# Layer 1's attention: one product of the ends of blocks 0 and 3 on GpSimd, and the gate multiplied last

## The chip, the core and the metric

The kernel runs on one core of a Trainium2 chip. A core has five engines that run side by side, each in its own order: TensorE (PE in the profile; PEld is its weight load), VectorE (DVE), ScalarE (ACT), GpSimd (POOL) and SyncE (SP). TensorE writes to PSUM, an accumulator memory in banks of 128 partitions x 512 fp32; all else is kept in SBUF. The metric is the device time of one execution in microseconds (us); the kernel before has a median of 3536.51 us over 3 runs (3531.72 to 3536.86).

## The reference, cut to what matters

Two layers over 2048 latent tokens on a 32 x 64 grid with 256 context tokens, model width 1024. The change lies in the second layer (layer 1): neighbourhood attention with 16 heads of 64, in which each query sees a window of 8 rows x 16 columns of the grid and all context tokens, then a gate.

```python
s_lat = einsum('bqhd,brkhd->bhqrk', qr, kb) * scale + bias        # window, with a table of biases
s_ctx = einsum('bqhd,bchd->bhqc', qr, k_ctx) * scale
p = softmax(concatenate([s_lat, s_ctx], -1))
o = einsum('bhqk,bkhd->bqhd', p_lat, vb) + einsum('bhqc,bchd->bqhd', p_ctx, v_ctx)
y = dot(o.reshape(..., 1024) * silu(z_x), w_out)
```

All is fp32. The projections and scores are computed with operands split into a high and a low part (names with h and l).

## The kernel before

Layer 1's attention (function odd_attention) works on one pair of the 16 heads at a time: eight turns j = 0 to 7, which this text calls heads 0 to 7. Queries are 4 blocks of 512 tokens (8 rows of the grid). In a head, 24 units follow each other: 8 for the context tokens (two per block) and 16 key tiles of 128 latent tokens (n = 0 to 15). A unit is

- eight score matmuls of TensorE (L1785) into a PSUM tile "st" of two banks; there are 2 such tiles, so that the scores of the next unit but one can only start when these have been read,
- for a key tile, additions of the bias table on VectorE (L1963), one to six of them for parts of the tile, from PSUM into an SBUF tile "opt" (11 of these),
- the exponential on ScalarE (L108, a helper through which all of ScalarE's work goes),
- some units later, the matmuls with the values into the output banks "o" (L1797 for context, L1815 for key tiles; 4 banks, one per block), and the sums of the exponentials "oacc" over key tiles, which GpSimd adds up (L1821; L1806 for the context, on VectorE for blocks 0 and 2, on GpSimd for 1 and 3).

When the last key tile of a block has been added, finish_blocks ends the block: TensorE sums oacc over the partitions (L1838, into an "st" tile), and ScalarE copies the result to an SBUF tile dc. From dc, which is minus twice the denominator, ScalarE makes rc, an approximate reciprocal by logarithm and exponential (tiles rl and opt). VectorE then takes four steps of 128 x 512:

- L1848: ln = dc x rc, both operands in SBUF,
- L1850: rc = rc x Z, both in SBUF, where Z is the gate (tiles os4 and ogate),
- L1854: o = (ln + 2) x o, in the output bank in PSUM; the factor ln + 2 corrects the reciprocal by one Newton step,
- L1855: rc = o x rc, from PSUM into SBUF.

A DMA issued by GpSimd (L1856) writes rc to HBM (RT1); the output projection after head 7 reads it.

finish_blocks is a generator: the attention loop takes one step of it per unit, so that its steps stand between those of the units. A scheduler then orders the instructions of each engine. Block 3 of a head is ended in the middle of the next head, and block 0 some 8 us later in its own head, so both ends stand close together. Block 2 of the head before is ended some 9 us ahead of its block 3, and block 1 of the head some 18 us behind its block 0. In head 7, blocks 2 and 3 are ended together, and VectorE and ScalarE also split the weights of the output projection.

Of the kernel before, what the change touches and what calls it, by code (L numbers as in the profile page):

```python
# [13 lines left out]
ALU = mybir.AluOpType  # L14
# [74 lines left out]
class Kern:  # L89
# [1630 lines left out]
    def odd_attention(self, out, pools, left, wout):  # L1720

        nc = self.nc
        self.RT1 = self.scr("RT1", (KD, P, SEQ), F32)
        NR, NC = (len(b) for b in BLOCKS["k"])
        with ExitStack() as es:
# [62 lines left out]
            def sums(acc, bb, n=1):  # L1788

                return [acc[bb // 2][:, i].rearrange("p r c -> p (r c)")[:, (bb % 2) * 512 : (bb % 2) * 512 + n * 512] for i in range(2)]  # L1790
# [41 lines left out]
            def finish_blocks(bbs, j, O, acc):  # L1832

                n, hf, o0 = len(bbs), bbs[0] // 2, bbs[0] % 2 * 512
                den = both()
                for b, bb in enumerate(bbs):
                    for i, a in enumerate(sums(acc, bb)):
                        mm = nc.tensor.matmul(den[i * 64 : i * 64 + 64, b, :], self.mtwos[:], a, start=True, stop=True)  # L1838
                dc = exps()
                self.act(dc[:, :n], den[:, :n])  # L1840
                yield mm
                ln = self.tl(lp, [P, 2, 512], "rl", bufs=1)
                self.act(ln[:, :n], dc[:, :n], AF.Ln, scale=-1.0)
                yield
                rc = exps()
                self.act(rc[:, :n], ln[:, :n], AF.Exp, scale=-1.0)
                yield
                nc.vector.tensor_tensor(out=ln[:, :n], in0=dc[:, :n], in1=rc[:, :n], op=ALU.mult)  # L1848
                flat = rc[:, :n].rearrange("p b c -> p (b c)")
                nc.vector.tensor_tensor(out=flat, in0=flat, in1=Z[j, hf][:, o0 : o0 + n * 512], op=ALU.mult)  # L1850
                yield
                for b, bb in enumerate(bbs):
                    o = O.pop(bb)[:].rearrange("p r c -> p (r c)")
                    nc.vector.scalar_tensor_tensor(out=o, in0=ln[:, b], scalar=2.0, in1=o, op0=ALU.add, op1=ALU.mult)  # L1854
                    nc.vector.tensor_tensor(out=rc[:, b], in0=o, in1=rc[:, b], op=ALU.mult)  # L1855
                (nc.sync if (j, bbs) == (7, [0]) else nc.gpsimd).dma_start(self.RT1[j, :, bbs[0] * 512 : (bbs[0] + n) * 512], flat)  # L1856

            def weights():

# [27 lines left out]
            Q, K, V, Z, tabs, raw = {}, {}, {}, {}, {}, {}  # L1887
# [15 lines left out]
            def flush(n):  # L1903

                mm = None
                for f, *a in pend[:n]:
                    mm = f(*a)
                del pend[:n]
                for x in late:
                    x[0] -= 1  # L1910
                for x in [x for x in late if x[0] <= 0]:
                    late.remove(x)
                    ends.append(finish_blocks(*x[1:]))
                    mm = next(ends[-1])
                    if x[1] == [0]:
                        for _ in ends.pop():
                            pass
                return mm
# [9 lines left out]
            for j in range(8):  # L1928
                OA[j] = {}, {}
                for s, (kind, n, u) in enumerate(units):  # L1930
                    g, c = divmod(n, 4)
# [21 lines left out]
                    else:  # L1953
# [7 lines left out]
                        for ro, ri, rn in pieces("k", 0, g, r0_, nr):  # L1961
                            for co, ci, cn in pieces("k", 1, c, c0, w):
                                bias = nc.vector.tensor_tensor(out=pt[:, :, ro : ro + rn, co : co + cn],  # L1963
                                                               in0=ps[:, :, ro : ro + rn, d + co : d + co + cn],
                                                               in1=tabs[j][:, :, ri : ri + rn, ci : ci + cn], op=ALU.add)
# [260 lines left out]
```

## Time and profile before

| | us |
|---|---|
| median of 3 runs (lowest, highest) | 3536.51 (3531.72, 3536.86) |
| the profiled execution's own time | 3539.31 |
| its span, first to last instruction | 3537.5 |
| layer 1's attention in it | about 2967 to 3364 |
| the output projection behind it | to the end |

The profile is of one execution. A row of a group shows line, engine, operation, output<-inputs by the program's names, shapes and count, then the total busy time in us and the mean of one in ns, then the idle time of the engine just ahead of these instructions and what ended it. A row of the order of time begins with start and length in us; in brackets stand the idle time ahead of it and its releaser, and x16 counts equal instructions in a row. In a row of a stretch of time, the busy time of each engine is followed by its count of instructions, and then come the clock granted to TensorE (1.00 is full speed), the busy share of the DMA engines and GB/s. Names of tiles stand without their buffer numbers.

### The profile page before, as it was taken

The numbers are of one execution on the slowest core, as the hardware profiler recorded it, in microseconds if no ns is written. First come the engines' busy times: TensorE is split into PE (matmuls) and PEld (weight loads), VectorE is DVE, ScalarE is ACT, GpSimd is POOL, SyncE is SP. The second block draws the span as 40 slices with busy tenths as digits, with TensorE's granted clock in tenths as the row PEclk, the third lists the DMA queues.
The fourth block names the chain that finished last, engine by engine and source line by source line (L and its number), as shares of the span: only waits on it lengthen the run. The fifth ranks groups of instructions, "written<-read, shape, count | busy, mean of one in ns | idle before, by whom it ended". The sixth has DMA issues, their size and how long they took to land. (4 is left out here: it accounts for less than half of the span.)

```text
span 3537.5 us, 54848 instructions
## 1 busy us (share of the span) xinstructions
PE 3442.3 (97%) x20228; PEld 2663.8 (75%) x20228; DVE 2438.7 (69%) x4522; ACT 1465.6 (41%) x2612; POOL 1052.0 (30%) x1295
## 2 busy tenths in 40 slices
PE   7999999999999999999999999999999999999899
PEld 6888987888896666665557878888788887555577
DVE  4677755888886777768876655455577884666865
ACT  4545552111113554546664344445422223555532
POOL 1343331111111333422211133333111114767611
PEclk9999999999999999999999999999999999999999
DMA  7555555233325242334525674445754546555374
GB/s 252 142 163 160 149 142 152 96 108 94 89 79 168 62 134 80 104 112 134 177 84 140 133 202 154 130 143 164 251 161 141 163 142 213 198 192 198 99 182 63
DMA packets 350111, 508.40 MB, mean 144 GB/s; under 512 B 32666, under 2 KB 233066, under 8 KB 342884
## 3 DMA queue, kind: packets, MB, share of 16 engines
q1 hardware_dynamic: 297364, 386.91, 35.9%
q0 software_dynamic: 29456, 82.14, 8.8%
q10 hardware_dynamic: 23024, 35.85, 3.0%
q8 instruction: 160, 2.62, 0.3%
q14 instruction: 107, 0.88, 0.1%
HBM read 325.99 MB, written 196.60 MB: 148 GB/s over the span
## 5 line engine op out<-in xcount | busy, mean ns | idle before, releaser
L706 DVE TENSOR_REDUCE mm<-mx 128x1 f32<-128x512 f32 (+1 forms) x656 | 389.3, 628 | 85.2 <-PE mx L705 78.2
L108 ACT ACTIVATE apt<-st 128x1024 f32<-128x1024 f32 (+1 forms) x296 | 300.2, 1015 | 303.2 <-PE st L1175 283.4
L1182 DVE TENSOR_TENSOR acc<-acc,apt 128x1024 f32<-128x1024 f32 x256 | 341.0, 1332 | 82.5 <-ACT apt L108 63.8
L1175 PE MATMUL st<-aq,akh 64*128 64x512 f32 x1728 | 312.0, 408 | 1.2 <-ACT apt L108 0.9
L1085 PE MATMUL av<-apt,av 128*64 128x512 f32 x1152 | 265.8, 598 | 0.0
L1821 POOL TENSOR_TENSOR oacc<-oacc,opt 128x528 f32<-128x528 f32 (+4 forms) x192 | 230.3, 1217 | 71.0 <-ACT opt L108 65.1
L705 PE MATMUL mx<-mk,mq 96*128 96x512 f32 (+1 forms) x656 | 236.0, 373 | 4.8 <-DMA mq<-QC 4.6
L1175 PE MATMUL st<-aq,akl 64*128 64x512 f32 (+1 forms) x1152 | 230.6, 390 | 0.0
L108 ACT ACTIVATE u<-gm 128x352 f32<-128x352 f32 (+1 forms) x140 | 68.6, 497 | 375.0 <-PE gm L133 207.1
L1703 DVE CUSTOM_DVE_ANT_1 mx<-mx,mtab 128x105 f32<-128x105 f32 (+14 forms) x576 | 183.1, 340 | 48.5 <-PE mx L1697 35.8
L1175 PEld LDWEIGHTS st<-aq,akh 64*128 64x128 f32 x1728 | 152.7, 185 | 82.7 <-ACT apt L108 28.8
L1963 DVE TENSOR_TENSOR opt<-st,tab 128x496 f32<-128x496 f32 (+16 forms) x288 | 124.5, 484 | 107.8 <-PE st L1785 106.1
L1085 PEld LDWEIGHTS av<-apt,av 128*64 128x64 f32 x1152 | 76.3, 136 | 135.3 <-issue 133.6
L108 ACT ACTIVATE opt<-opt 128x930 f32<-128x930 f32 (+9 forms) x130 | 104.5, 806 | 161.2 <-DVE opt L1963 155.1
L705 PEld LDWEIGHTS mx<-mk,mq 96*128 96x128 f32 x656 | 121.6, 189 | 17.0 <-issue 5.1
L1175 PEld LDWEIGHTS st<-aq,akl 64*128 64x128 f32 (+1 forms) x1152 | 112.1, 184 | 22.9
L1785 PE MATMUL st<-qh,kh 64*128 64x512 f32 (+6 forms) x384 | 85.1, 438 | 32.1 <-DVE opt L1963 25.8
L1785 PEld LDWEIGHTS st<-qh,kh 64*128 64x128 f32 x384 | 37.7, 190 | 102.4 <-issue 48.6
L220 POOL TENSOR_TENSOR oss<-oss,mhalf 128x8 f32<-128x8 f32 x68 | 112.6, 1656 | 5.4
L1552 DVE TENSOR_TENSOR onat<-gm,oss 128x512 f32<-128x512 f32 x68 | 46.9, 690 | 95.8 <-POOL oss L220 95.8
L131 PE MATMUL gm<-w1h,hhi 128*128 128x512 f32 x280 | 112.0, 400 | 0.2 <-ACT ovz L108 0.2
L133 PE MATMUL gm<-w1h,hlo 128*128 128x512 f32 x280 | 110.0, 393 | 0.0
(778 smaller groups left out, 9724.6 us busy)
## 6 DMA issues: line engine op xcount, KB each, us to landing
H<-x ACTq DMA_DIRECT2D x32, 512.0 KB
adaw<-ada_w SPq DMA_DIRECT2D x64, 256.0 KB
wraw<-w_od SPq DMA_DIRECT2D x64, 256.0 KB
K1t<-okt POOLq DMA_DIRECT2D x16, 1024.0 KB, 6.6
x<-H SPq DMA_DIRECT2D x31, 512.0 KB
mtab<-rpb_q SPq DMA_DIRECT2D x16, 899.0 KB
x<-xin SPq DMA_DIRECT2D x18, 512.0 KB
x<-xin POOLq DMA_DIRECT2D x18, 512.0 KB, 5.3
```

The lines of the kernel that those rows point to most:

```text
L108: return self.nc.scalar.activation(out, in_, func, **kw)
L131: self.nc.tensor.matmul(out, lh(k), rh(k), start=start and j == 0, stop=False)
L220: return g.tensor_tensor(out=out, in0=out, in1=self.mhalf[:, : shp[1]], op=ALU.pow)
L705: mm = nc.tensor.matmul(ps[:, :w], q[:A_QK, (t % 6) * P : (t % 6) * P + P], k[:A_QK, k0 : k0 + w], start=True, stop=True)
L706: nc.vector.tensor_reduce(out=m[:, t, n : n + 1], in_=ps[:, :w], axis=AX.X, op=ALU.max)
L1085: mm = nc.tensor.matmul(O[j, nb][i * 64 : i * 64 + 64, :w], V[j, kt // TT][:, kt % TT, i * 64 : i * 64 + 64], pts[:, i, :w], start=n == 0, ...
L1175: mm = nc.tensor.matmul(ps[:, o // 64, :w], k[o : o + r, kb, kq], Q[o : o + r, qb, :w], start=m == 0, stop=m == 4)
L1182: added = nc.vector.tensor_tensor(out=acc[:, :, :w], in0=a[:, :, :w], in1=pts[:, :, :w], op=ALU.add)
L1703: nc.vector.tensor_tensor_reduce(out=s, in0=s, in1=tb[:, ri : ri + rn, ci : ci + cn], scale=1.0, scalar=-3e38, op0=ALU.add, op1=ALU.max, a ...
L1785: mm = nc.tensor.matmul(ps(i), ones[s] if k is None else k[s, ks], qs(q[s]), start=n == 0, stop=n == 3)
L1821: nc.gpsimd.tensor_tensor(out=a, in0=a, in1=pts[:, :, a0 - r0 : a1 - r0, :], op=ALU.add)
L1963: bias = nc.vector.tensor_tensor(out=pt[:, :, ro : ro + rn, co : co + cn], in0=ps[:, :, ro : ro + rn, d + co : d + co + cn], in1=tabs[j][: ...
```

## The change

For blocks 0 and 3 of heads 0 to 6, which are 14 of the 31 block ends, the product ln = dc x rc is issued on GpSimd instead of VectorE. In all block ends the gate's product is taken out of its place ahead of the two steps on the output bank. Instead the bank is first multiplied by rc in place, and the gate is multiplied last, out of the bank into rc.

```diff
-                nc.vector.tensor_tensor(out=ln[:, :n], in0=dc[:, :n], in1=rc[:, :n], op=ALU.mult)
-                flat = rc[:, :n].rearrange("p b c -> p (b c)")
-                nc.vector.tensor_tensor(out=flat, in0=flat, in1=Z[j, hf][:, o0 : o0 + n * 512], op=ALU.mult)
+                near = nc.gpsimd if bbs in ([0], [3]) and j < 7 else nc.vector
+                near.tensor_tensor(out=ln[:, :n], in0=dc[:, :n], in1=rc[:, :n], op=ALU.mult)
                 yield
                 for b, bb in enumerate(bbs):
                     o = O.pop(bb)[:].rearrange("p r c -> p (r c)")
                     nc.vector.scalar_tensor_tensor(out=o, in0=ln[:, b], scalar=2.0, in1=o, op0=ALU.add, op1=ALU.mult)
-                    nc.vector.tensor_tensor(out=rc[:, b], in0=o, in1=rc[:, b], op=ALU.mult)
-                (nc.sync if (j, bbs) == (7, [0]) else nc.gpsimd).dma_start(self.RT1[j, :, bbs[0] * 512 : (bbs[0] + n) * 512], flat)
+                    nc.vector.tensor_tensor(out=o, in0=o, in1=rc[:, b], op=ALU.mult)
+                    nc.vector.tensor_tensor(out=rc[:, b], in0=o, in1=Z[j, hf][:, o0 + b * 512 : o0 + b * 512 + 512], op=ALU.mult)
+                (nc.sync if (j, bbs) == (7, [0]) else nc.gpsimd).dma_start(self.RT1[j, :, bbs[0] * 512 : (bbs[0] + n) * 512], rc[:, :n].rearrange("p b c -> p (b c)"))
```

In the changed kernel the first product is line L1849, the three steps on the bank are L1853, L1854 and L1855, and the DMA stays L1856. The order of TensorE's and ScalarE's instructions stays as it was. On VectorE, where block 3 of head 1 is ended in the middle of head 2 (rl_29205 is ln, opt_29189 dc, opt_29219 rc, ogate the gate, o_28845 the bank; the first L1963 rows are the bias of the key tile ahead, opt_29283 that of the next):

```order
 L1963 TENSOR_TENSOR opt_29227<-st_29226,tab_28558 128x2x15x16
 L1963 TENSOR_TENSOR opt_29227<-st_29226,tab_28558 128x2x15x7
-L1848 TENSOR_TENSOR rl_29205<-opt_29189,opt_29219 128x512
-L1850 TENSOR_TENSOR opt_29219<-opt_29219,ogate_29024 128x512
-L1854 SCALAR_TENSOR_TENSOR o_28845<-rl_29205,o_28845 128x512
-L1855 TENSOR_TENSOR opt_29219<-o_28845,opt_29219 128x512
+L1853 SCALAR_TENSOR_TENSOR o_28845<-rl_29205,o_28845 128x512
+L1854 TENSOR_TENSOR o_28845<-o_28845,opt_29219 128x512
+L1855 TENSOR_TENSOR opt_29219<-o_28845,ogate_29024 128x512
 L1963 TENSOR_TENSOR opt_29283<-st_29282,tab_28558 128x2x15x8
 L1963 TENSOR_TENSOR opt_29283<-st_29282,tab_28558 128x2x15x16
```

VectorE goes straight from the bias to L1853, which needs GpSimd's ln, and the next bias stands behind the three steps. A little later on VectorE, at the end of block 0 of head 2 (rl_29317 is ln, os4 the gate, o_29058 the bank):

```order
 L1963 TENSOR_TENSOR opt_29327<-st_29326,tab_28558 128x2x465
-L1848 TENSOR_TENSOR rl_29317<-opt_29315,opt_29319 128x512
 L1963 TENSOR_TENSOR opt_29339<-st_29338,tab_28558 128x2x465
-L1850 TENSOR_TENSOR opt_29319<-opt_29319,os_5038_29158 128x512
-L1854 SCALAR_TENSOR_TENSOR o_29058<-rl_29317,o_29058 128x512
-L1855 TENSOR_TENSOR opt_29319<-o_29058,opt_29319 128x512
+L1853 SCALAR_TENSOR_TENSOR o_29058<-rl_29317,o_29058 128x512
+L1854 TENSOR_TENSOR o_29058<-o_29058,opt_29319 128x512
+L1855 TENSOR_TENSOR opt_29319<-o_29058,os_5038_29157 128x512
 L1963 TENSOR_TENSOR opt_29356<-st_29355,tab_28558 128x2x15x16
```

The second 2 x 465 bias now follows the first one directly, ahead of everything that needs ln. On GpSimd, the changed kernel's order from the end of block 3 of head 1 to the end of block 0 of head 2 (oacc_5010 and oacc_5045 are the sums of blocks 0, 1 and of blocks 2, 3 of head 2):

```order
L1821 TENSOR_TENSOR oacc_5010_29008<-oacc_5010_29008,opt_29208 128x2x11x31
L1821 TENSOR_TENSOR oacc_5045_29203<-oacc_5045_29203,opt_29192 128x2x4x31
L1849 TENSOR_TENSOR rl_29205<-opt_29189,opt_29219 128x512
L1821 TENSOR_TENSOR oacc_5010_29008<-oacc_5010_29008,opt_29227 128x2x11x23
L1821 TENSOR_TENSOR oacc_5045_29203<-oacc_5045_29203,opt_29208 128x2x4x31
L1821 TENSOR_TENSOR oacc_5045_29203<-oacc_5045_29203,opt_29227 128x2x4x23
L1856 DMA RT<-opt_29219 128x512
L1806 TENSOR_TENSOR oacc_5045_29203<-opt_29241,opt_29272 128x2x512
L1821 TENSOR_TENSOR oacc_5010_29008<-oacc_5010_29008,opt_29283 128x2x3x24
L1821 TENSOR_TENSOR oacc_5045_29203<-oacc_5045_29203,opt_29283 128x2x12x24
L1849 TENSOR_TENSOR rl_29317<-opt_29315,opt_29319 128x512
L1821 TENSOR_TENSOR oacc_5010_29008<-oacc_5010_29008,opt_29327 128x2x3x31
```

The two L1849 rows are new; the DMA L1856 stood ahead of the 2 x 4 x 23 addition before, and all other rows keep their order.

## The prediction

> **What bounds the kernel now.** I read the busy time of the stage that the change touches first, then its groups by shape, and last its order of time around the places where TensorE stands still. In layer 1's attention TensorE is busy for 364.56 of 397 us (the first number after the comma; VectorE's is the third, GpSimd's the fifth, the granted clock 0.96):
>
> ```profile
> 2967.00:3364.00 397.00, 364.56 (x3161) 224.22 (x3161) 268.59 (x433) 220.05 (x298) 282.43 (x237) 0.96 0.51 182
> ```
>
> So a microsecond saved on VectorE or GpSimd counts only where TensorE waits for it. Groups by shape (count, busy time, mean ns, idle time of the engine ahead and who ended it) show one such place:
>
> ```profile
> L1785 PE MATMUL st<-qh,kh 64*128 64x264 f32 x32 | 6.7, 416 | 14.9 <-DVE opt L1963 14.9
> L1848 DVE TENSOR_TENSOR rl<-opt,opt 128x512 f32<-128x512 f32 x30 | 48.1, 1604 | 37.6 <-ACT opt L108 37.6
> L1855 DVE TENSOR_TENSOR opt<-o,opt 128x512 f32<-128x512 f32 x32 | 22.0, 690 | 0.9
> ```
>
> The score matmuls of one key tile waited 14.9 us for VectorE's bias addition L1963. And L1848, the product that the change moves, takes 1604 ns on average, while L1855, as large but with one operand in PSUM, takes 690. The order of time in the middle of head 2, where block 3 of head 1 and then block 0 of head 2 are finished (start, length):
>
> ```profile
> 3083.97 1.50 POOL L1821 TENSOR_TENSOR oacc<-oacc,opt 128x682 f32<-128x682 f32 x1
> 3084.38 1.64 DVE L1848 TENSOR_TENSOR rl<-opt,opt 128x512 f32<-128x512 f32 x1
> 3085.43 1.13 POOL L1821 TENSOR_TENSOR oacc<-oacc,opt 128x248 f32<-128x248 f32 x1
> 3086.51 1.63 POOL L1821 TENSOR_TENSOR oacc<-oacc,opt 128x506 f32<-128x506 f32 x1
> 3087.03 0.68 DVE L1854 SCALAR_TENSOR_TENSOR o<-rl,o 128x512 f32<-128x512 f32 x1
> 3087.74 0.69 DVE L1855 TENSOR_TENSOR opt<-o,opt 128x512 f32<-128x512 f32 x1
> 3088.09 0.66 POOL L1821 TENSOR_TENSOR oacc<-oacc,opt 128x248 f32<-128x248 f32 x1
> 3088.35 0.96 DVE L1963 TENSOR_TENSOR opt<-st,tab 128x240 f32<-128x240 f32 x2
> 3088.73 0.55 POOL L1856 DMA_DIRECT2D RT<-opt  x1
> 3089.30 0.56 POOL L1821 TENSOR_TENSOR oacc<-oacc,opt 128x184 f32<-128x184 f32 x1
> 3089.34 0.81 ACT L108 ACTIVATE opt<-opt 128x720 f32<-128x720 f32 x1 [1.19 <-DVE opt L1963]
> 3089.80 2.39 POOL L1806 TENSOR_TENSOR oacc<-opt,opt 128x1024 f32<-128x1024 f32 x1
> 3090.00 0.49 PE L1785 MATMUL st<-qh,kh 64*128 64x480 f32 x2
> 3090.12 0.60 ACT L108 ACTIVATE opt<-st 128x512 f32<-128x512 f32 x1
> 3092.15 3.95 POOL L1821 TENSOR_TENSOR oacc<-oacc,opt 128x144 f32<-128x144 f32 x4
> 3092.25 4.40 DVE L1848 TENSOR_TENSOR rl<-opt,opt 128x512 f32<-128x512 f32 x1
> 3092.61 1.41 POOL L1821 TENSOR_TENSOR oacc<-oacc,opt 128x576 f32<-128x576 f32 x1
> 3096.57 1.11 DVE L1963 TENSOR_TENSOR opt<-st,tab 128x930 f32<-128x930 f32 x1
> 3097.74 0.39 PE L1785 MATMUL st<-qh,kh 64*128 64x264 f32 x2 [2.98 <-DVE opt L1963]
> 3098.44 3.02 PE L1815 MATMUL o<-opt,ov 128*64 128x72 f32 x24
> ```
>
> At 3092.25 L1848 stands still for 4.40 us: GpSimd's four additions end at 3096.10 (3092.15 + 3.95) and only then does it run its usual 0.6. The bias addition behind it comes at 3096.57, and TensorE sits idle for 2.98 us until its score bank is read. L1854 and L1855, with one operand in PSUM, take 0.68 and 0.69 beside a running GpSimd. Five heads have this gap (5 x 2.98 = 14.9); heads 0 and 5 have smaller ones there:
>
> ```profile
> 3003.80 0.43 PE L1785 MATMUL st<-qh,kh 64*128 64x352 f32 x2 [1.57 <-DVE opt L1963]
> 3244.47 0.43 PE L1785 MATMUL st<-qh,kh 64*128 64x352 f32 x2 [0.78 <-DVE opt L1963]
> 3256.58 0.50 PE L1785 MATMUL st<-qh,kh 64*128 64x512 f32 x2 [0.93 <-DVE opt L1963]
> ```
>
> There is a second price. Right behind each of the five gaps the granted clock (third number from the end) is 0.50 (the first and fourth of five stretches, and their sum):
>
> ```profile
> 3050.56:3053.97 3.41, 3.41 (x28) 2.74 (x24) 2.30 (x8) 1.40 (x2) 3.39 (x5) 0.50 0.17 65
> ...
> 3193.92:3200.74 6.82, 5.83 (x44) 4.76 (x46) 4.54 (x11) 2.38 (x3) 4.69 (x6) 0.50 0.10 38
> ...
> sum 23.89, PE 21.56 PEld 17.23 DVE 17.69 ACT 9.03 POOL 17.66; mean PE 4.31 PEld 3.45 DVE 3.54 ACT 1.81 POOL 3.53
> ```
>
> **The change, part by part.**
>
> 1. Block 0's L1848 leaves VectorE (heads 0 to 6). The 4.40 us go, and the second 930-wide L1963 now stands ahead of the wait. Gain on TensorE: the five gaps, 14.9 us.
>
> 2. With them goes the halved clock. TensorE was busy for 21.56 us at half speed; at full speed that is 10.8. Gain 10.8; 0 if another idle stretch halves the clock there again.
>
> 3. What takes their place: VectorE is in order, and L1853 now waits for the GpSimd product L1849, with the next bias additions queued behind it. L1849's length is not in this trace. The nearest rows are GpSimd's products of the same shape in layer 0:
>
> ```profile
> L1010 POOL TENSOR_TENSOR rc<-rc,azt 128x512 f32<-128x512 f32 x16 | 20.7, 1292 | 129.2 <-DVE rc L1008 129.2
> L850 POOL TENSOR_TENSOR gat<-gat,ge 128x512 f32<-128x512 f32 x18 | 36.6, 2032 | 112.7 <-DVE gat L848 112.7
> 2991.67 1.16 POOL L1821 TENSOR_TENSOR oacc<-oacc,opt 128x506 f32<-128x506 f32 x1
> ```
>
> I take 1.29 (the lower bound is 1.16, a slightly narrower addition); 2.03 is the upper end, from a line that runs beside VectorE products, while here VectorE will be waiting. The Trainium skill says, in "GPSIMD Engine Reference", section 3.1, that an fp32 tensor-tensor takes GpSimd about twice VectorE's time (1.96x); 1292 against 690 here is 1.87x, and 1.96 x 690 would make it 1.35 and the sum below 0.8 us worse.
>
> Block 3, in head 2's times. GpSimd's 682 ends at 3085.47. Its 248 is no longer disturbed (0.66 instead of 1.13): 3086.14. L1849: 3087.46. Three VectorE steps (0.71, 0.71, 0.61 from start to start; the third multiplies the gate out of PSUM and is priced as L1855) end at 3089.55, where L1963 began at 3088.35 before: 1.2 later. It ends near 3090.55, TensorE wanted its bank at 3090.00 and waits 0.6. ScalarE's 0.81 and then 0.60 move to 3092.0, which holds the second score tile by another 0.4. GpSimd gets back 0.47 on the 248 and 0.47 on the 506 (1.16, not 1.63), which pays most of L1849.
>
> Block 0: GpSimd goes on from 3087.46 with 1.16, 0.66, 0.56, a DMA issue of 0.55, 2.39, then the 144 and 576 wide additions (0.46 to the 576's start, and 1.41), then L1849: 3096.1. Three steps end at 3098.2, the next L1963 pair at 3099.2. TensorE, 1.0 late, now at full clock, has run the 264-wide tile and its 24 matmuls (3.02 becomes 1.6) by 3098.1 and waits 1.1 to 1.2. Together 2.2 us a head, in six heads (1 to 6): 13.2 us lost. The bounds: none of it, if GpSimd runs ahead by that much; 13.2 + 14 x 0.74 = 23.6 with 2.03, since each of the 14 products (two in each of seven heads) moves a TensorE wait by its own length.
>
> 4. Head 0 has block 0 alone: 1.57 becomes some 0.5, a gain of 1.1. Head 5's 0.78 and 0.93 fall under point 3's waits: gain 1.7.
>
> 5. Head 7 ends block 3 of head 6. There a gap of 2.04 follows an L1848 among VectorE's weight work:
>
> ```profile
> 3341.68 0.49 PE L1785 MATMUL st<-qh,kh 64*128 64x480 f32 x2 [2.04 <-DVE opt L1963]
> ```
>
> Part of it goes; against it the output bank is held one step (0.69) longer for the gate. I take 0, with 2 us either way.
>
> 6. The gate product itself: one VectorE step out, one in, 0.69 each. In blocks 1 and 2 it moves behind the bias addition, hidden as before by TensorE. The DMA of L1856 moves behind one 0.56 addition on GpSimd; layer 1's outputs are read only at the end: 0.
>
> Sum: -14.9 - 10.8 + 13.2 - 1.1 - 1.7 + 0 = -15.3 us. Against the profiled execution's 3539.31 that is 3524.0; the median of the runs is 2.8 lower, so 3521.2.
>
> **A rule weighed.** In the trace 1.59 us of idle TensorE in a 3.42 us stretch (1.83 busy) left the clock at 1.00 and 1.64 (1.77 busy) was followed by 0.50:
>
> ```profile
> 3313.38:3316.80 3.42, 1.83 (x14) 0.81 (x14) 2.85 (x5) 3.06 (x5) 2.65 (x3) 1.00 0.35 129
> 3340.69:3344.10 3.41, 1.77 (x14) 1.32 (x16) 3.41 (x4) 2.44 (x4) 3.39 (x3) 1.00 0.20 77
> 3344.10:3347.52 3.42, 3.42 (x13) 0.98 (x10) 3.42 (x3) 0.90 (x2) 1.52 (x2) 0.50 0.70 219
> ```
>
> The new waits are 0.6 + 0.4 together and 1.2 alone, under that. The Trainium skill ("TensorE: Matmul & The Clock Gate", section "Why this matters for your kernels") asks only for no idle gaps over about 3 us; by that the 2.98 us gaps would cost no clock, which is rival E's sum, within 0.2%. The trace disagrees with it: all five gaps of 2.98 are followed by 0.50.
>
> **Rivals.** 0.2%, or 7 us, is about what a measurement of this kernel tells from no change.
> - A, no change. L1849 takes 2.03, as in L850's row: 14 x 0.74 = 10.4 us more, -4.9: 3531.6. For it: such a row exists. Against: 1292 in sixteen products of the same form.
> - B, slower: the new waits halve the clock. It decides once block 3's waits pass 1.6 us in one stretch of 3.4: with 2.03 they are 1.7. Then each of six heads loses half of 3.4 to 6.8 us, 1.7 to 3.4, on top of A: +5 to +15, 3542 to 3552.
> - C, better: GpSimd's queue has slack that I don't see and the new waits vanish: -28.5, 3508.
> - D, the change does not do what it says: the 4.40 are not GpSimd's doing, and block 0's steps in PSUM stall as long: -1, 3535. Against it stand L1855's mean of 690 above and L1854 (minimum, median, maximum in ns):
>
> ```profile
> L1854 DVE SCALAR_TENSOR_TENSOR o<-rl,o x32: 681/683/691, 3001.4 to 3386.5; 128x512 f32<-128x512 f32 x32
> ```
>
> - E, the halved clock has another cause than the gaps and stays: point 2 is 0, -15.3 + 10.8 = -4.5, 3532. Against it: the clock rows just above.
>
> **How the numbers follow.** Forecast (-22 to -8) 0.68, A 0.10, B 0.06, C 0.10, D 0.03, E 0.03. Faster: forecast, C and the near edge of A, 0.80; same 0.14; slower 0.06. The range reaches from near C to A's 3531.6: 3509 to 3532; the forecast's own is 3514.5 to 3528.5.
>
> **What would show it.** L1849 on GpSimd 14 times at 1.2 to 1.4 us; no 4.4 us on VectorE; the 14.9 of the 264-wide score tile gone, with waits of 0.4 to 1.2 for L1963 at the 480- and 352-wide tiles; clock 1.00 from 3045 to 3290; heads 3 us shorter. I am wrong if L1849 is over 1.7, or if clock 0.50 still follows the middle of a head.

## The result and the profile after

The changed kernel takes 3519.81 us in the median of 5 runs (3519.53 to 3523.02), the kernel before 3536.51 in 5 runs beside it (3531.72 to 3536.86). The ratio is 0.9959, with a 95% interval of 0.9944 to 0.9973: 16.7 us faster (14.5, at the middle of that ratio), and the prediction was 15.3 faster, 3521.2.

The profiled execution took 3519.81 with a span of 3518.0, which is 19.5 less than the span before. Not all of it lies where the change is. The groups of one line give the start of the first and of the last of the score matmuls L1785; before:

```profile
L1785 PE MATMUL st<-qh,kh x384: 281/443/660, 2967.2 to 3364.0; 64*128 64x512 f32 x64, 64*128 64x360 f32 x32, 64*128 64x480 f32 x32, 64*128 64x288 f32 x16
```

and after:

```profile
L1785 PE MATMUL st<-qh,kh x384: 278/432/766, 2961.5 to 3345.0; 64*128 64x512 f32 x64, 64*128 64x360 f32 x32, 64*128 64x480 f32 x32, 64*128 64x288 f32 x16
```

Layer 1's attention begins 5.7 us earlier, in code that the change doesn't touch; that part differs by some us from one execution to the next (2958.9 to 2967.5 in the eleven traces of this study). So all traces are compared below by **the stage**, from the first L1785 to the end of the span: 570.4 us before (3537.5 - 2967.2) and 556.6 after, 13.8 less, against the 15.3 of the prediction's sum. Up to the last score matmul of head 7 the two traces have TensorE's and ScalarE's instructions in the same order; behind it, in the output projection, some of them have changed places.

The busy times of the engines in the attention after (order of columns as in the prediction's first row: TensorE, its weight load, VectorE, ScalarE, GpSimd, then the granted clock):

```profile
2961.00:3345.50 384.50, 356.63 (x3169) 219.71 (x3169) 235.06 (x419) 220.45 (x298) 292.56 (x251) 0.98 0.54 188
```

VectorE is 33 us less busy (268.59 before), GpSimd 10 us more, and TensorE's clock is 0.98 instead of 0.96. Two groups of score matmuls by shape before (busy, mean ns, then the idle time ahead and who ended it):

```profile
L1785 PE MATMUL st<-qh,kh 64*128 64x480 f32 x64 | 14.9, 459 | 4.7 <-DVE opt L1963 2.6 <-ACT opt L108 1.3
L1785 PE MATMUL st<-qh,kh 64*128 64x352 f32 x32 | 8.0, 491 | 6.2 <-DVE opt L1963 6.2
```

and the groups after:

```profile
L1849 POOL TENSOR_TENSOR rl<-opt,opt 128x512 f32<-128x512 f32 x14 | 18.5, 1319 | 0.0
L1849 DVE TENSOR_TENSOR rl<-opt,opt 128x512 f32<-128x512 f32 x16 | 15.4, 963 | 36.8 <-ACT opt L108 36.8
L1853 DVE SCALAR_TENSOR_TENSOR o<-rl,o 128x512 f32<-128x512 f32 x32 | 22.0, 689 | 33.9 <-POOL rl L1849 33.9
L1785 PE MATMUL st<-qh,kh 64*128 64x480 f32 x64 | 15.4, 474 | 7.8 <-DVE opt L1963 6.8 <-ACT opt L108 0.5
L1785 PE MATMUL st<-qh,kh 64*128 64x352 f32 x32 | 7.2, 432 | 13.5 <-DVE opt L1963 13.5
L1785 PE MATMUL st<-qh,kh 64*128 64x264 f32 x32 | 5.5, 338 | 0.7 <-DVE opt L1963 0.7
```

The 14.9 us at the 264-wide score tile are 0.7. In their place TensorE waits longer at the 352-wide tile (13.5 for 6.2) and the 480-wide one (7.8 for 4.7); heads 1 to 6 have 8.6 and 5.5 of these waits, and had 0.8 at each before. Ahead of them VectorE's L1853 waits for GpSimd's product (33.9). Rows from the order of time in the middle of head 2, the same place as in the prediction:

```profile
3076.96 1.29 POOL L1849 TENSOR_TENSOR rl<-opt,opt 128x512 f32<-128x512 f32 x1
3078.28 0.70 DVE L1853 SCALAR_TENSOR_TENSOR o<-rl,o 128x512 f32<-128x512 f32 x1 [3.55 <-POOL rl L1849]
3079.82 0.69 DVE L1855 TENSOR_TENSOR opt<-o,ogate 128x512 f32<-128x512 f32 x1
3080.42 0.96 DVE L1963 TENSOR_TENSOR opt<-st,tab 128x240 f32<-128x240 f32 x2
3081.53 0.49 PE L1785 MATMUL st<-qh,kh 64*128 64x480 f32 x2 [0.85 <-DVE opt L1963]
...
3082.73 2.37 DVE L1963 TENSOR_TENSOR opt<-st,tab 128x930 f32<-128x930 f32 x2 [1.34 <-PE st L1785]
3083.75 1.87 POOL L1821 TENSOR_TENSOR oacc<-oacc,opt 128x144 f32<-128x144 f32 x2
3085.56 1.29 POOL L1849 TENSOR_TENSOR rl<-opt,opt 128x512 f32<-128x512 f32 x1
3086.89 0.69 DVE L1853 SCALAR_TENSOR_TENSOR o<-rl,o 128x512 f32<-128x512 f32 x1 [1.79 <-POOL rl L1849]
3089.03 1.74 DVE L1963 TENSOR_TENSOR opt<-st,tab 128x480 f32<-128x480 f32 x6
3090.11 0.43 PE L1785 MATMUL st<-qh,kh 64*128 64x352 f32 x2 [1.42 <-DVE opt L1963]
```

The 4.40 us are gone, and each product on GpSimd is followed, some 2 us later, by a TensorE wait: 0.85 behind block 3, 1.42 behind block 0.

### The profile page after: what moved, and what is told of

Its sections match the earlier page's. It is cut to its first block, busy times and chain, and to the rows that moved or that the text cites. A ratio compares the mean times of both kernels' runs of the same rounds, so it can differ in the third digit from the quotient of the medians.

```text
span 3518.0 us, 54816 instructions
## 1 busy us (share of the span) xinstructions
PE 3431.9 (98%) x20228; PEld 2656.4 (76%) x20228; DVE 2405.5 (68%) x4509; ACT 1466.8 (42%) x2612; POOL 1061.2 (30%) x1309
## 4 chain that ended last, share of the span: by engine, by line
PE 78%; DVE 6%; POOL 5%; DMA 5%; ACT 3%; issue 2%; SPq 1%; DVEq 0%; ACTq 0%; POOLq 0%
PE gm L133 10%; PE gm L131 10%; PE gm L132 10%; PE st L1175 10%; PE av L1085 7%; PE mx L705 4%; PE st L1785 2%; PE pu L1364 2%; PE o L1364 2%; POOL oacc L1821 2%; PE st L1364 1%; PE pj L1364 1%; PE mx L1697 1%; PE o L1815 1%; DMA adaw<-ada_w 1%
## 5 line engine op out<-in xcount | busy, mean ns | idle before, releaser
L1821 POOL TENSOR_TENSOR oacc<-oacc,opt 128x528 f32<-128x528 f32 (+4 forms) x192 | 221.6, 1171 | 48.1 <-ACT opt L108 42.7
L1963 DVE TENSOR_TENSOR opt<-st,tab 128x496 f32<-128x496 f32 (+16 forms) x288 | 124.3, 485 | 94.6 <-PE st L1785 93.6
L705 PEld LDWEIGHTS mx<-mk,mq 96*128 96x128 f32 x656 | 121.6, 189 | 17.5 <-issue 5.3
L1785 PE MATMUL st<-qh,kh 64*128 64x512 f32 (+6 forms) x384 | 83.4, 429 | 27.4 <-DVE opt L1963 22.7
L131 PE MATMUL gm<-w0h,hhi 128*128 128x512 f32 x272 | 109.6, 403 | 0.0
```

Source lines behind the costliest of these rows:

```text
L131: self.nc.tensor.matmul(out, lh(k), rh(k), start=start and j == 0, stop=False)
L705: mm = nc.tensor.matmul(ps[:, :w], q[:A_QK, (t % 6) * P : (t % 6) * P + P], k[:A_QK, k0 : k0 + w], start=True, stop=True)
L1821: nc.gpsimd.tensor_tensor(out=a, in0=a, in1=pts[:, :, a0 - r0 : a1 - r0, :], op=ALU.add)
```

## The experiments

All are edits of the changed kernel but one, which says so. The table takes the stage apart, from the trace of each: the length of head 0, of heads 1 to 6 and of head 7 (from the first L1785 of a head to that of the next, for head 7 to its last), and the remainder to the end. In heads 1 to 6, *idle* is the sum of TensorE's idle times over 0.05 us, *half* is half of its busy time in stretches with a granted clock of 0.50, and *rest* is what is left of the length.

| us | stage | head 0 | heads 1-6 | idle | half | rest | head 7 | to the end |
|---|---|---|---|---|---|---|---|---|
| before | 570.4 | 41.4 | 291.5 | 17.6 | 10.8 | 263.0 | 64.4 | 173.0 |
| changed | 556.6 | 40.6 | 280.6 | 14.8 | 1.7 | 264.1 | 62.9 | 172.5 |
| 1 gate last, no GpSimd | 563.7 | 40.7 | 290.0 | 17.5 | 11.4 | 261.0 | 60.5 | 172.4 |
| 2 gate first, GpSimd | 596.8 | 40.6 | 317.5 | 41.5 | 13.5 | 262.5 | 65.6 | 173.0 |
| 3 block 0 alone | 548.6 | 40.5 | 274.1 | 10.5 | 1.7 | 261.8 | 60.4 | 173.6 |
| 4 block 3 alone | 567.9 | 40.6 | 293.6 | 23.0 | 6.8 | 263.8 | 61.3 | 172.3 |
| 5 additions left out | 537.6 | 40.2 | 263.8 | 2.2 | 0.0 | 261.7 | 61.4 | 172.2 |
| 6 VectorE, in steps | 570.4 | 40.8 | 296.8 | 21.9 | 13.9 | 261.1 | 60.5 | 172.3 |
| 7 both, in steps | 553.2 | 40.9 | 278.3 | 12.9 | 0.0 | 265.4 | 61.5 | 172.4 |
| 8 block 0, in steps | 546.3 | 40.9 | 271.8 | 9.0 | 0.0 | 262.8 | 61.1 | 172.4 |
| 9 block 0, later | 538.3 | 39.8 | 264.3 | 0.8 | 0.0 | 263.5 | 60.4 | 173.8 |

Idle and half explain the large differences in heads 1 to 6; the rest lies between 261.0 and 265.4, and the cause of that spread was not traced. Head 7 moves by a few us between kernels, in part with the halved clock in it (1.5 to 5.9 us). Each row is one execution, in experiments 3, 4, 8 and 9 one that took 2.4 to 5.3 us less than the median of its kernel's runs, so that a difference of a few us between two rows is not shown by the table alone.

**1. The gate alone.** The swap of the gate's product without GpSimd.

```diff
-                near = nc.gpsimd if bbs in ([0], [3]) and j < 7 else nc.vector
+                near = nc.vector
```

> The gate is multiplied last, out of the block's bank, but every product of two SBUF operands stays on VectorE. The stage is counted from the first score matmul of layer 1 to the end of the span: 570.4 us before, 556.6 us after. Theory (the engine of block 0's product is what counts): the product of block 0 still takes 4.4 us on VectorE beside GpSimd's four additions, five TensorE gaps of about 2.98 us stay, and the clock is halved behind them; stage 568 to 572, time 3532 to 3540, the same as before. Rival (the swap of the gate product brings the gain): stage about 557, time about 3520.

Measured: 3531.22 us, ratio 0.9984 (0.9975 to 0.9993); stage 563.7. Neither theory's stage: of the 13.8 us 6.7 are there (by the times 5.6, with 2.5 to 8.8 as the interval), and the other half is not. The order of time at the end of block 0 of head 2:

```profile
3088.48 3.97 POOL L1821 TENSOR_TENSOR oacc<-oacc,opt 128x144 f32<-128x144 f32 x4
3088.67 4.34 DVE L1849 TENSOR_TENSOR rl<-opt,opt 128x512 f32<-128x512 f32 x1
...
3092.93 1.11 DVE L1963 TENSOR_TENSOR opt<-st,tab 128x930 f32<-128x930 f32 x1
...
3094.10 0.59 PE L1785 MATMUL st<-qh,kh 64*128 64x264 f32 x2 [2.91 <-DVE opt L1963]
```

The held product, the gap and the halved clock stay (idle 17.5, half 11.4), so what heads 1 to 6 lack against the changed kernel (290.0 for 280.6) is what GpSimd's part brings. What the swap brings lies elsewhere: in head 0 (0.8), in the rest of heads 1 to 6 (2.0 less) and in head 7 (3.9 less, of which 1.5 is clock). What makes up the last two was not traced, but head 7 is 64.4 and 65.6 long in the two kernels with the gate in its old place, and 60.4 to 62.9 in the nine with the gate last. Head 0 shows how a part of it comes about. Before, its gate product L1850 was held, and longer than the product that the change moves (1.29):

```profile
2999.27 4.19 POOL L1821 TENSOR_TENSOR oacc<-oacc,opt 128x744 f32<-128x744 f32 x3
...
2999.78 1.69 DVE L1850 TENSOR_TENSOR opt<-opt,os 128x512 f32<-128x512 f32 x1
```

Out of the bank it takes 0.69, and the 1.57 us that TensorE waited there are 0.74 in this kernel.

**2. GpSimd with the gate in its old place**, an edit of the kernel before:

```diff
-                nc.vector.tensor_tensor(out=ln[:, :n], in0=dc[:, :n], in1=rc[:, :n], op=ALU.mult)
+                near = nc.gpsimd if bbs in ([0], [3]) and j < 7 else nc.vector
+                near.tensor_tensor(out=ln[:, :n], in0=dc[:, :n], in1=rc[:, :n], op=ALU.mult)
```

> The first products of blocks 0 and 3 on GpSimd as in the changed kernel, but the gate keeps its old place: rc x Z on VectorE, both operands in SBUF, ahead of the two steps on the bank (L1851 here). Stage from the first score matmul of layer 1 to the end: 570.4 us before, 556.6 changed, 563.7 with the gate last and no GpSimd. Theory (a product of two SBUF operands is held by GpSimd's additions, the gate's as the first one, so step 6 was wrong with its 0): at the ends of block 0 the gate's product takes 1.7 us or more and the gap of head 0 is 1.5 or more instead of 0.69; stage 561 to 568, time 3524 to 3531. Rival (the gate product costs 0.69 in either place, as step 6 has it): stage 556 to 558, time 3519 to 3521.

Measured: 3565.38 us, ratio 1.0076 (1.0063 to 1.0089): slower than before by 27 us, and stage 596.8. The theory was right that the gate's product is held too, but its size was far too small: it took head 0's 1.7 us as the price, and heads 1 to 6 pay more. Rows from the order of time at the end of block 0 of head 2 (here L1851 is the gate's product and L1964 the bias):

```profile
3097.75 1.89 POOL L1821 TENSOR_TENSOR oacc<-oacc,opt 128x144 f32<-128x144 f32 x2
3099.60 1.28 POOL L1849 TENSOR_TENSOR rl<-opt,opt 128x512 f32<-128x512 f32 x1
3100.85 4.18 POOL L1821 TENSOR_TENSOR oacc<-oacc,opt 128x186 f32<-128x186 f32 x4
3100.91 4.67 DVE L1851 TENSOR_TENSOR opt<-opt,os 128x512 f32<-128x512 f32 x1 [1.81 <-POOL rl L1849]
...
3107.91 0.66 PE L1785 MATMUL st<-qh,kh 64*128 64x352 f32 x2 [5.22 <-DVE opt L1964]
```

With the first product on GpSimd, the next SBUF-by-SBUF product on VectorE inherits the hold: GpSimd's next four additions start 0.06 us ahead of it, and it ends 0.55 after they do (3105.58; they end at 3105.03). To that comes the wait of 1.81 for GpSimd, and the gap is 5.22. Apart, one half of the change is worth some 5.6 us and the other costs 27; together they make the gain.

**3. Block 0 alone on GpSimd.**

```diff
-                near = nc.gpsimd if bbs in ([0], [3]) and j < 7 else nc.vector
+                near = nc.gpsimd if bbs == [0] and j < 7 else nc.vector
```

> Only the ends of block 0 take their product on GpSimd; those of block 3 take it on VectorE as before; the gate stays last. Theory: the two waits behind block 3's end (0.83 + 0.08 us in each of heads 1 to 6, 5.5 us in all) are VectorE's wait for GpSimd's product and vanish; the wait behind block 0's end (1.42) stays: stage about 551, time about 3514. Rival (the waits behind block 3's end are there for another reason, the longer chain of steps out of the bank): stage 556 to 557, time about 3520.

Measured: 3518.34 us, ratio 0.9947 (0.9934 to 0.9960); stage 548.6. The waits behind block 3 are gone, as the theory has it: idle falls from 14.8 to 10.5, and heads 1 to 6 by 6.5. One wait per head is left, 1.62 to 1.67 behind block 0 (1.41 to 1.43 in the changed kernel). The medians show less of it (1.5 us, by the ratios 4; the intervals overlap), and head 7 was shorter in this trace by 2.5. Experiments 7 and 8 show it more clearly.

**4. Block 3 alone on GpSimd** (`bbs == [3]` in the same line).

> Only the ends of block 3 take their product on GpSimd; block 0's stays on VectorE; the gate last. Stage 563.7 us with the gate last and no GpSimd. Theory (the gain on GpSimd is block 0's alone, block 3's product costs the waits of 0.83 + 0.08 us in each of heads 1 to 6): the product of block 0 is still held for over 4 us, gaps of 2 to 3 us with the halved clock stay, and 5 us of waits come on top: stage 566 to 574, time 3533 to 3543. Rival (taking block 3's 1.64 us from VectorE is a gain by itself): stage 555 to 562, time 3520 to 3529.

Measured: 3537.52 us, ratio 0.9999 (0.9990 to 1.0008); stage 567.9. As the theory has it: the 0.85 us behind block 3 and a gap of 2.7 behind block 0 stand in each of heads 1 to 6 (idle 23.0). Of the change, the part on block 3 costs time: it takes 1.64 us from VectorE at a place where TensorE had not waited, and puts a wait there.

**5. The additions left out.** All products on VectorE, the gate last, and

```diff
+                    if j == 7 or n not in (8, 9):
                         nc.gpsimd.tensor_tensor(out=a, in0=a, in1=pts[:, :, a0 - r0 : a1 - r0, :], op=ALU.add)
...
-                self.act(dc[:, :n], den[:, :n])
+                self.act(dc[:, :n], den[:, :n], AF.Identity, bias=self.mhalf[:, 0:1])
```

> All products on VectorE, the gate last, but GpSimd's additions of key tiles 8 and 9 are left out in heads 0 to 6, so that those terms are missing from the softmax sums (a constant of 0.5 is taken off dc to keep it negative). Theory (the 4.4 us of block 0's product on VectorE are GpSimd's additions beside it): the product of block 0 takes 0.7 to 1.2 us, the six gaps of 2.9 and the halved clock behind them are gone, heads 1 to 6 take 44 to 45 us each, stage 540 to 548. Rival (the product is slow there for another reason, such as its operands' place or a wait for ScalarE): it still takes over 3 us and the gaps stay, stage 560 to 566.

Measured: 3501.52 us in its one run; stage 537.6, a little below the theory's range. The end of block 0 of head 2 (here L1850 is the first product, L1822 an addition):

```profile
3080.59 0.68 DVE L1850 TENSOR_TENSOR rl<-opt,opt 128x512 f32<-128x512 f32 x1
...
3083.41 2.13 POOL L1822 TENSOR_TENSOR oacc<-oacc,opt 128x186 f32<-128x186 f32 x2 [2.94 <-ACT opt L108]
...
3085.37 0.43 PE L1785 MATMUL st<-qh,kh 64*128 64x352 f32 x2 [0.19 <-DVE opt L1964]
```

The same product at the same place in VectorE's order takes 0.68 instead of 4.34 when GpSimd has nothing to add (it waits 2.94 for ScalarE), and with it the gaps and the halved clock are gone. So the 4.4 us are GpSimd's additions, and rival D falls.

**6. All on VectorE, the end of block 0 in steps.** Block 0's end used to be run through at once as soon as it was due; here its steps are handed out one per unit, like those of the other blocks. The edit is that of experiment 1 and

```diff
                     ends.append(finish_blocks(*x[1:]))
                     mm = next(ends[-1])
-                    if x[1] == [0]:
-                        for _ in ends.pop():
-                            pass
```

> All products on VectorE, the gate last, but the end of block 0 handed out one step at a time between the biases: its product stands behind the bias of the next key tile instead of ahead of it. Theory (GpSimd must take block 0's product, since its additions hold it wherever it stands on VectorE): it takes 1.5 to 4.5 us at its new place, TensorE waits 1 to 3 us a head there; stage 553 to 565, time 3517 to 3530. Rival (only the place counted: behind the bias nobody waits for the held product): stage 540 to 549, time 3504 to 3512, and no GpSimd was needed.

Measured: 3537.44 us, ratio 1.0000 (0.9991 to 1.0009); stage 570.4, worse than the theory's range. The product is held at its new place just as long:

```profile
3088.68 7.67 POOL L1821 TENSOR_TENSOR oacc<-oacc,opt 128x144 f32<-128x144 f32 x8
...
3092.37 4.53 DVE L1849 TENSOR_TENSOR rl<-opt,opt 128x512 f32<-128x512 f32 x1
...
3097.86 0.66 PE L1785 MATMUL st<-qh,kh 64*128 64x352 f32 x2 [3.56 <-DVE opt L1960]
```

Eight additions follow each other from 3088.68 to 3096.35, and the product ends 0.55 later, at 3096.90. Where it stands in VectorE's order does not help it while GpSimd's queue is full.

**7. Both on GpSimd, block 0 in steps** (the edit of the last diff alone).

> Both products on GpSimd as in the changed kernel, but the end of block 0 is handed out one step at a time between the biases, as the ends of the other blocks are, and not drained at once. VectorE's first step after the product then stands behind further biases. Theory (the 1.42 us are VectorE standing in order before a product that was issued just ahead): they vanish in heads 1 to 6, 8.5 us, the 0.83 + 0.08 behind block 3 stay; stage about 548, time about 3511. Rival (the later release of block 0's bank makes the context products of the next head wait as long): stage 555 to 560, time 3519 to 3523.

Measured: 3519.99 us, ratio 0.9955 (0.9942 to 0.9967); stage 553.2. The theory was wrong: the 1.42 turned into waits of 0.91 to 0.98 and 0.28 at the sums of block 1 (L1838), and the median is that of the changed kernel. Only the halved clock in head 4 is gone.

**8. Block 0 alone on GpSimd, in steps** (experiment 3's line and the last diff).

> Only block 0's product on GpSimd, and the end of block 0 handed out one step at a time between the biases. Theory: no step of VectorE waits for GpSimd any longer than a bias covers; the 0.83 + 0.08 and the 1.42 us are both gone from heads 1 to 6 (14 us), and so is the halved clock in head 4 (about 1.6): stage 541 to 544, time 3504 to 3508. Rivals: the bank is released too late (stage 550 to 556), or shorter waits add up within one stretch of the clock and it is halved all the same (stage 545 to 550).

Measured: 3511.95 us, ratio 0.9930 (0.9917 to 0.9942); stage 546.3, in the range of the second rival but not for its reason: no stretch of heads 1 to 6 is at half clock. The end of block 0 of head 2 (here L1960 is the bias):

```profile
3086.49 1.28 POOL L1849 TENSOR_TENSOR rl<-opt,opt 128x512 f32<-128x512 f32 x1
...
3087.80 0.70 DVE L1853 SCALAR_TENSOR_TENSOR o<-rl,o 128x512 f32<-128x512 f32 x1 [1.19 <-POOL rl L1849]
...
3089.94 1.76 DVE L1960 TENSOR_TENSOR opt<-st,tab 128x496 f32<-128x496 f32 x4
3091.01 1.08 PE L1838 MATMUL st<-oacc,mtwos 128*64 128x512 f32 x4 [1.17 <-DVE opt L1960]
```

Nor is it the bank's release. The reason is the one found in the changed kernel: a VectorE step that waits for GpSimd, with a bias behind it that TensorE needs, now for L1838. Experiments 7 and 8 differ by block 3's product alone: without it on GpSimd the ratio is 0.9930 for 0.9955, and the intervals only touch.

**9. Block 0 later.** Experiment 8, and one more unit between the product and the steps on the bank:

```diff
                 near.tensor_tensor(out=ln[:, :n], in0=dc[:, :n], in1=rc[:, :n], op=ALU.mult)
                 yield
+                if near is nc.gpsimd:
+                    yield
```

> Only block 0's product on GpSimd, its end handed out one step at a time, and the three steps on block 0's bank moved one unit further back, behind the first bias additions of the next key tile. Theory: in the kernel with the end of block 0 in steps, the 1.17 + 0.34 us that are left in heads 1 to 6 are the sums of block 1 (L1838) waiting for a score bank whose bias stands on VectorE behind a step that waits 1.19 us for GpSimd; with that bias ahead they fall to 0 to 0.4: stage 537 to 541, time 3501 to 3507. Rival (VectorE's work, not its order, is what is late there; or the product comes so late that the next bias waits): stage 545 to 549, time 3510 to 3514.

Measured: 3504.23 us, ratio 0.9903 (0.9889 to 0.9916); stage 538.3, as the theory has it. This version beats both kernels, the changed one by 0.4% in the medians and 0.6% by the two ratios. Heads 1 to 6 have 0.8 us of idle time left in all. Their busy times before (columns as above):

```profile
3008.62:3300.08 291.46, 273.71 (x2400) 168.78 (x2401) 195.28 (x324) 161.78 (x216) 210.98 (x182) 0.96 0.51 185
```

and in this kernel:

```profile
2998.61:3262.91 264.30, 263.49 (x2400) 161.93 (x2401) 178.01 (x319) 159.90 (x216) 215.66 (x187) 1.00 0.58 203
```

The clock is 1.00, and TensorE is busy for 263.49 of 264.30 us: what is left of these heads is its own work.

## Why the prediction was right, point by point

**1, the five gaps: right.** They are gone (14.9 us to 0.7 at the 264-wide tile). Experiments 1 and 5 show the cause as told, block 0's first product held beside GpSimd's additions.

**2, the halved clock: right, 1.7 us too much.** Half-speed work in heads 1 to 6 fell from 10.8 to 1.7 us, not to 0. In head 4 the clock was halved behind a new wait that the prediction called safe; the prediction named a clock of 0.50 there as a sign of being wrong, and it came in one head of six. The stretches with that wait in head 1 and in head 4 after the change, each with the stretch behind it:

```profile
3041.70:3045.10 3.40, 1.97 (x24) 1.52 (x20) 3.06 (x9) 1.43 (x2) 3.39 (x5) 1.00 0.00 0
3045.10:3048.50 3.40, 3.35 (x40) 1.95 (x36) 1.27 (x4) 2.15 (x3) 3.32 (x4) 1.00 0.20 77
3181.60:3185.00 3.40, 1.97 (x22) 1.42 (x20) 3.10 (x9) 1.43 (x2) 3.39 (x5) 1.00 0.00 0
3185.00:3188.40 3.40, 3.40 (x26) 2.33 (x28) 0.97 (x3) 1.55 (x2) 3.32 (x4) 0.50 0.23 84
```

Both have TensorE busy for 1.97 of 3.40 us, idle for 1.43, and only the second is followed by 0.50. So the line that the prediction drew between 1.59 and 1.64 is a zone. Over the eleven traces of this study, of the stretches of the attention at full clock, all 41 with more than 1.93 us of idle TensorE were followed by 0.50, 10 of the 28 with 1.43 to 1.93, and none of the some 1100 with less. The Trainium skill ("TensorE: Matmul & The Clock Gate", section "Why this matters for your kernels") asks for no idle gaps over about 3 us; here gaps of less than half of that cost clock.

**3, the new waits: right, a little small.** GpSimd's product has a mean of 1319 ns (1.29 was taken). A head has 0.85 + 0.08 + 1.42 = 2.35 us of waits where 0.6 + 0.4 + 1.15 was worked out, and heads 1 to 6 are 1.8 us shorter on average, not 3. Experiments 3 and 9 show that the waits come from VectorE's order, as told: without block 3's product its wait is gone, and with the bias ahead of the waiting step so is block 0's.

**4, heads 0 and 5: the size right, the cause of head 0 wrong.** Head 0 gained 0.9 (41.45 to 40.56 us; 1.1 was forecast), its wait falling to 0.69, but experiment 1 gives nearly all of that without GpSimd: the longer hold there was that of the gate's product. Head 5 had no gap of 2.98 before, and it alone got longer (44.8 to 46.4 us). Its rows before show why it had none:

```profile
3236.82 2.39 POOL L1806 TENSOR_TENSOR oacc<-opt,opt 128x1024 f32<-128x1024 f32 x1
...
3239.12 0.68 DVE L1848 TENSOR_TENSOR rl<-opt,opt 128x512 f32<-128x512 f32 x1
3239.17 7.04 POOL L1821 TENSOR_TENSOR oacc<-oacc,opt 128x144 f32<-128x144 f32 x6
```

VectorE's product started 0.05 us ahead of the first addition and took 0.68. In head 2 it started 0.10 behind it and took 4.40. In head 5 of experiment 1 it started 0.04 behind it (3234.13, the addition at 3234.09) and took 4.47. The 0.93 that the prediction counts to head 5 stands in head 6, which begins at 3249.3: there block 1's product, which stays on VectorE, took 1.73 us from 3253.04. In the changed kernel it took 1.08 and TensorE did not wait.

**5, head 7: within its 2 us.** 64.4 became 62.9; the gap of 2.04 is 1.78 after. A gain was not forecast, and by the lengths under experiment 1 the gate's new place brings one here.

**6, the gate product at 0: the step that failed.** It was priced as one step out and one in, 0.69 each. By itself the swap is worth about 5.6 us (experiment 1), and with the first product on GpSimd it is worth 40 us of the stage (596.8 against 556.6). The gate's product was short at that place before because GpSimd's queue had run dry behind the held product. In head 2 the additions had ended at 3096.10, and the next one came at 3098.85:

```profile
3097.61 0.68 DVE L1850 TENSOR_TENSOR opt<-opt,os 128x512 f32<-128x512 f32 x1
```

The sum came out near all the same, since the replay under point 3 priced the changed kernel's steps, with the gate out of PSUM.

**The sum.** Heads 1 to 6: idle 17.6 to 14.8, 2.8 less (3.4 by points 1, 3 and head 5), half 9.1 less (10.8), rest 1.0 more (not forecast, and not traced to a cause). Head 0 gives 0.9, head 7 1.6 and the remainder 0.5: 13.8 in all, for 15.3. So the nearness of the sum is in part luck: heads 1 to 6 gave 10.9 of the 14.2 us that were forecast for them, and 2.1 came from head 7 and the remainder, for which nothing was. The profiled executions differ by 5.7 more, ahead of the stage.

**The rivals.** A and B needed a product of 2.03 us; it takes 1.3, and B's halved clock came in one head. C's vanishing waits did not come by themselves; experiment 9 makes them vanish by order, and lands at 3504. E falls with experiments 5 and 9: without gaps, no stretch of heads 1 to 6 is at half clock.

## What to carry to other kernels

Where VectorE's product of two SBUF operands stands beside a full GpSimd queue, move the operands and not only the instruction: take one from PSUM, and look which SBUF-by-SBUF step stands next in line, since it inherits the hold. Move to GpSimd only the product whose hold TensorE waits for (block 0's; block 3's was held for 1.64 us where TensorE did not wait, and to move it cost time), and put ahead of the step that waits for it, on the in-order engine, whatever TensorE needs next. Price TensorE's waits by where they fall as well as by their length: 1.4 to 1.9 us in one stretch of the clock cost another 1.7 or more in 10 of 28 cases.

## What the runs showed of the hardware

A held product on VectorE waits in two ways. Most often it ends 0.55 us after the addition that was running when it started: block 3's 1.64 us in the prediction's rows, from 3084.38 to 3086.02, 0.55 behind the 682-wide addition's end at 3085.47, and the 248-wide addition behind that one pays, 1.13 us instead of 0.66. At block 0 it does not get in between the additions and ends 0.55 after the last of a row of them (4.40 us before, 4.67 in experiment 2, 4.53 in experiment 6). The Trainium skill ("SBUF — State Buffer", sections "SBUF: two separate sides" and "Who interferes with whom") says that a VectorE instruction with two SBUF inputs contends with a GpSimd instruction that reads SBUF, and that whichever starts first gets the pair of ports that they share for the whole instruction; the 0.68 and 4.47 us of the two heads 5, with starts 0.05 ahead and 0.04 behind, agree, and one instruction's hold explains the 1.64. The 4.40, held over four instructions, goes beyond that sentence. What decides between the two ways stays open: no run here varied the spacing of GpSimd's instructions.
